# A hybrid decoder step: a projection's remainders on VectorE, its stores a block later, two rooms exchanged and one room each for two sums of weights

## The chip, the cores and the metric

The kernel runs on one core of one Trainium2 chip. A core has a matrix engine (TensorE, PE in the profile, with its weight loads as PEld), three engines for elementwise work (VectorE or DVE, ScalarE or ACT, GpSimd or POOL) and SyncE (SP), which only issues DMAs here. Each engine runs its own list of instructions in order and waits on semaphores for the others. The metric is the device time of one execution in microseconds (us). Three runs of the kernel before gave 1149.54, 1150.51 and 1150.65 us; the median is 1150.51 us.

## The reference

The reference is one step of a decoder with one layer: 1024 new tokens of a prompt behind 16 meta tokens, and 8 running sequences with 4 new tokens each, 1072 columns in all; the model width is 1024. In short:

```python
u = rmsnorm(h, g) @ w_in                  # q, k, v, gate, conv input, dt
mix = concat(window_attention(q, k, v), mamba2_ssd(conv(xbc), dt))
h = h + norm_and_gate(mix) @ w_out        # output projection
a = relu(rmsnorm(h, g2) @ w_up) ** 2      # 1024 -> 4096
h = h + a @ w_down                        # 4096 -> 1024
y = rmsnorm(h, g_final)
```

All of it is in float32, and the caches and states are outputs too.

## The kernel before, in words

Activations lie with features on the 128 partitions and tokens along the free dimension. Every float32 operand `x` of a large product is split into a rounded `hi` and a remainder `lo = x - hi`, and a product is three products on PE: `hi*hi`, `hi*lo`, `lo*hi`. So each block of weights goes through a load (SyncE), a cast to `hi` (ScalarE) and a subtraction for `lo` (VectorE or GpSimd) before PE can use it. These are `load_wout` (lines 240, 243 and 244 in it) for the output projection and `split_w` (lines 1252 and 1253) for the MLP. Tiles called `whi`, `wlo` and `w7x` are six rooms that take the split weights in turn.

The stages, by the time in the trace: input projection and attention (to about 305 us), the state-space part together with the first half of the output projection (to about 414 us), the second half of the projection, the MLP's first layer (466 to about 800 us), its second layer (to about 1134 us), and the last norm.

The output projection's columns come in three chunks (two of them 288 and 384 wide make up columns 0 to 671, the third has 384). Blocks `m` of 128 features are counted 0 to 7. In the second half, `wout_stream` runs through m and the first two chunks: `mixer_half` adds the product to `ha`, ScalarE squares it, GpSimd sums the squares in `sq`. The sum is stored to `he` in DRAM by SyncE (line 1012), and `gained` (line 970) multiplies `ha` in place by the norm's gain, which has to wait until that store has read it. `Ahead` loads two blocks of weights ahead. Then the loop `for m in range(8)` does the third chunk in the same way with VectorE for its sums and remainders, and between its blocks runs the norms of chunks 0 and 1 in steps (`norms2`, `token_norm`): sum over features on PE (`c`), the reciprocal root, a diagonal matrix `dg` on VectorE (line 1223), and its spread over partitions by PE.

The MLP's layers use a scheme with seven products instead of eight for 2 x 2 blocks (j = 1 to 7); some need sums or differences of weight blocks, made in `prep_up`: `S = a21 + a22` for j=5, `S - a11` for j=6, `a11 - a21` for j=7, `a12 - S` for j=3. The 16 output pairs p run one after the other. For the first six ("early" pairs), j=1 and j=2 are computed ahead of the rest, while the second half of the operands is still being made; their relu-squared result `b11` is stored from GpSimd's queue (line 1342), and the main steps (5, 6, 7, 4, 3) follow later. In a main step, j=6 and j=7 go on adding to the same two banks; after each, ScalarE copies the banks out (`copies`, line 1310, tiles `s2` and `s3`). The next product into a bank has to wait for that copy. VectorE adds copies and banks to the outputs `u` (line 1315). `prepare` keeps the weights of four steps ahead.

The rooms `s2` and `s3` have one buffer each and serve `b11` of the early pairs first. `S` has two buffers; `a11 - a21` is written into the place of the loaded `a21`.

A scheduler orders each engine's instructions within what the dependences allow, so the order in the trace is not the order of the code. `final_last` at the end of the program normalises the last columns and has six idle matmuls ahead of the last spread.

Of the kernel before, what the change touches and what calls it, by code (L numbers as in the profile page):

```python
# [9 lines left out]
F32 = mybir.dt.float32  # L10
# [181 lines left out]
def body(ctx: ExitStack, tc: tile.TileContext, xT, xm, win, wdt, wo, wu, wd, ck, cv, sc, st, sT, vec, consts,  # L192
# [54 lines left out]
    class Ahead:  # L247
# [9 lines left out]
        def next(self):  # L257
            while self.fns and len(self.got) <= self.n:
                self.more()
            return self.got.pop(0)  # L260
# [633 lines left out]
    kv_s.close()  # L894


    weights = Ahead([lambda m=m, half=half: load_wout(m, half) for half in range(2) for m in range(8)], 2)
    weights.more()
    hd = dram.tile([128, 8, TM], F32, name="hd")
    he = dram.tile([128, 8, TM], F32, name="he")  # L900
# [67 lines left out]
    def gained(m, out, x):  # L968

        ACT.activation(out=out, in_=x, func=AF.Copy, scale=vec[:, V_G2 + m:V_G2 + m + 1])  # L970
# [3 lines left out]
    def wout_stream():  # L974

        ws = {}
        for m, ch in [(0, 0), (0, 1), (1, 0), (1, 1), (0, 2), (1, 2)] + [(m, ch) for m in range(2, 8) for ch in range(3)]:
            c0, cw = CM[ch]
            if m not in ws:
                ws[m] = weights.next()  # L980
            hb = sp.tile([128, 384], F32, name="hb", tag="hb", bufs=3)[:, :cw]
            SP.dma_start(out=hb, in_=xm[:, 8 * c0 + m * cw:8 * c0 + (m + 1) * cw])
            ps = gps()
            gemm(ps[:, :cw], ws[m], X[ch])
            DVE.tensor_tensor(out=hb, in0=hb, in1=ps[:, :cw], op=ALU.add)
            SP.dma_start(out=hd[:, m, c0:c0 + cw], in_=hb)
            yield
        acta_s.close()
        opb = act_s.enter_context(pool("opb", side="right"))

        ha = xn["ha"] = opb.tile([128, 8, TM], F32, name="ha")
        c2 = CM[2][0]
        first = [load_kept(0, ch, sp) for ch in range(2)]
        SP.dma_start(out=ha[:, 1], in_=hd[:, 1])
        SP.dma_start(out=ha[:, 2], in_=hd[:, 2])
        SP.dma_start(out=ha[:, 0, c2:], in_=hd[:, 0, c2:])
        for m in range(3, 8):
            SP.dma_start(out=ha[:, m], in_=hd[:, m])
        sq01 = opb.tile([128, CM[2][0]], F32, name="sq01")
        sq.update({ch: sq01[:, CM[ch][0]:CM[ch + 1][0]] for ch in range(2)})  # L1000
        pieces = [(m, ch) for m in range(8) for ch in range(2)]
        for m, ch in pieces:
            c0, cw = CM[ch]
            if ch == 0:
                w = weights.next()
            hb = ha[:, m, c0:c0 + cw] if m else first[ch]
            mixer_half(m, ch, w, hb, sp, POOL)
            if m == 0:
                SP.dma_start(out=he[:, m, c0:c0 + cw], in_=hb)
                gained(m, ha[:, m, c0:c0 + cw], hb)  # L1010
            elif ch == 1:
                SP.dma_start(out=he[:, m, 0:c2], in_=ha[:, m, 0:c2])
                if m > 1:
                    gained(m - 1, ha[:, m - 1, 0:c2], ha[:, m - 1, 0:c2])
            yield
        gained(7, ha[:, 7, 0:c2], ha[:, 7, 0:c2])

    def xcols(i):
        if i == 0:
# [255 lines left out]
    def prep_up(p, j, first):  # L1275

        g = p if p < NPRE and j in (1, 2) else NPRE + p
        if first:
            load_up(g + 2)
            if g == len(groups) - 1:  # L1280
                load_first((0, 1))
        a11, a12 = raws[g, 0][:, 0:4], raws[g, 0][:, 4:8]
        if g >= NPRE:
            a21, a22 = raws[g, 1][:, 0:4], raws[g, 1][:, 4:8]
        tt = DVE.tensor_tensor
        if j == 5:
            S_[p] = pu.tile([128, 4, 128], F32, name="S", tag="S", bufs=2)
            tt(out=S_[p], in0=a21, in1=a22, op=ALU.add)
        elif j == 6:
            tt(out=S_[p], in0=S_[p], in1=a11, op=ALU.subtract)  # L1290
        elif j == 7:
            tt(out=a21, in0=a11, in1=a21, op=ALU.subtract)
        elif j == 3:
            tt(out=a12, in0=a12, in1=S_[p], op=ALU.subtract)
        src = {5: lambda: S_[p], 1: lambda: a11, 2: lambda: a12, 6: lambda: S_[p], 7: lambda: a21, 4: lambda: a22, 3: lambda: a12}[j]()
        wts[p, j] = split_w(pu, "w7x", src)

    OPN = {1: "b11", 2: "b21", 3: "b22", 4: "t4", 5: "t1", 6: "t2", 7: "t3"}
# [32 lines left out]
    def run_up(p, j):  # L1331
        pre = p < NPRE
        if pre and j == 1:
            chain[p, "a"] = [bank("b" if p % 2 else "g") for _ in range(2)]
            product(chain[p, "a"], p, 1, True)
            s_[p, 1] = copies("s1", chain[p, "a"], 2)
            POOL.dma_start(out=s1d[p], in_=s_[p, 1])
        elif pre and j == 2:
            product(chain[p, "a"], p, 2, False)
            b = pu.tile([128, 2, TQ], F32, name="b11", tag="s2" if p % 2 else "s3", bufs=1)  # L1340
            relu2_of(b, chain[p, "a"])
            POOL.dma_start(out=u7[p][:, 4], in_=b.rearrange("p c t -> p (c t)"))
        elif j == 5:
            us[p] = pu.tile([128, 4, TH], F32, name="u", tag="u", bufs=2)
            if pre:
                s_[p, 1] = pu.tile([128, 2, TQ], F32, name="s1", tag="s1", bufs=2)
                SP.dma_start(out=s_[p, 1], in_=s1d[p])
                chain[p, "a"] = [bank("g") for _ in range(2)]
                for c in range(2):
                    ACT.copy(out=chain[p, "a"][c][:, :TQ], in_=s_[p, 1][:, c])  # L1350
                SP.dma_start(out=us[p][:, 0], in_=u7[p][:, 4])
            chain[p, "b"] = [bank("b") for _ in range(2)]
            product(chain[p, "b"], p, 5, True)
        elif j == 1:
            chain[p, "a"] = [bank("g") for _ in range(2)]
            product(chain[p, "a"], p, 1, True)
            s_[p, 1] = copies("s1", chain[p, "a"], 2)
        elif j == 2:
            cc = [bank("c") for _ in range(2)]
            product(cc, p, 2, True)  # L1360
            sums(quad(p, 0), cc, s_[p, 1])
            relu2(us[p][:, 0], 0)
        elif j in (6, 7):
            product(chain[p, "a"], p, j, False)
            s_[p, j] = copies("s2" if j == 6 else "s3", chain[p, "a"])
            if j == 7:
                sums(quad(p, 2), chain[p, "b"], s_[p, 7])
                relu2(us[p][:, 2], 1)
        elif j == 4:
            product(chain[p, "a"], p, 4, False)  # L1370
            relu2_of(quad(p, 1), chain[p, "a"])
        else:
            product(chain[p, "b"], p, 3, False)
            sums(quad(p, 3), chain[p, "b"], s_[p, 6])
            relu2(us[p][:, 3], 1)
            u, t = us[p], pu.tile([128, 4, TH], F32, name="t", tag="x", bufs=2)
            tt = DVE.tensor_tensor
            tt(out=t[:, 0], in0=u[:, 3], in1=u[:, 0], op=ALU.subtract)
            tt(out=t[:, 2], in0=u[:, 2], in1=u[:, 3], op=ALU.subtract)
            tt(out=t[:, 1], in0=u[:, 2], in1=t[:, 0], op=ALU.subtract)  # L1380
            tt(out=t[:, 3], in0=u[:, 1], in1=t[:, 1], op=ALU.subtract)
            a = 1 if pre else 0
            POOL.dma_start(out=u7[p][:, 4 + a:7], in_=u[:, a:3])  # L1383
            POOL.dma_start(out=u7[p][:, 0:4], in_=t)
# [71 lines left out]
    for m in range(8):  # L1456
        w = ahead
        if m < 7:
            ahead = weights.next()
        mixer_half(m, 2, w, bs[:, m, c2:], nw, DVE)  # L1460
        POOL.dma_start(out=he[:, m, c2:], in_=bs[:, m, c2:])
        gained(m, xn["b22" if m > 3 else "b12"][:, m % 4, c2 - TH:], bs[:, m, c2:])
        if m < 6:
            next(norms2[m // 3], None)
        if m in (0, 2):
            operand(xa, "b21" if m else "b11")
            split_op("b21" if m else "b11", bs[:, 2 * m:2 * m + 4, 0:TH])
        elif m == 3:
            for n, name in enumerate(("b12", "b22")):
                ACT.copy(out=xn[name][:, :, 0:CM[2][0] - TH], in_=bs[:, 4 * n:4 * n + 4, TH:c2])  # L1470
            prepare(1)
        elif m == 4:
            DVE.tensor_tensor(out=xn["b11"], in0=xn["b12"], in1=bs[:, 0:4, 0:TH], op=ALU.subtract)
            prepare(2)
        elif m == 5:
            ACT.copy(out=xn["b21"], in_=bs[:, 4:8, 0:TH])
# [238 lines left out]
    def final_last():  # L1715
# [17 lines left out]
        pt = sum_tokens("c", q2[:, 3])  # L1733

        for _ in range(6):
            mm(idle2[:, 0:128], ones, ones, True, True)
        rs = hpool.tile([128, 3], F32, name="rs3", tag="rs3", bufs=2)
        DVE.scalar_tensor_tensor(out=rs, in0=pt[:, 0:3], scalar=1.0 / D, in1=part, op0=ALU.mult, op1=ALU.add)
        POOL.tensor_tensor(out=rs, in0=rs, in1=nhalf[:, 0:3], op=ALU.pow)
# [67 lines left out]
```

## Time and profile before

| | us |
|---|---|
| median of three runs | 1150.51 |
| the profiled execution | 1149.81 |
| its span on the engines | 1147.9 |
| PE busy | 1115.6 |
| VectorE busy | 842.9 |
| ScalarE busy | 568.7 |
| GpSimd busy | 243.9 |

The profile is of one execution. Its span is counted from the first to the last instruction; 1.9 us lie around it. The mean granted clock of PE is 0.993 of its full speed. In the timeline, a row gives start and duration in us, the engine, the line, the operation with its output and input tiles, the shape and, in brackets, how long the engine had been idle before it and what released it. A line 202 is the helper that issues every matmul, so matmuls are told apart by their tiles. A line "SPq" or "POOLq" stands for the issuing of a DMA.

### The profile page before, as it was taken

How to read it: one execution, taken by the hardware profiler on the slowest of the kernel's cores; microseconds unless marked ns; L12 is line 12 of the kernel's file. 1: busy time of each engine (PE TensorE's matmuls, PEld its weight loads, DVE VectorE, ACT ScalarE, POOL GpSimd, SP SyncE). 2: the span in 40 equal slices, each digit the busy share in tenths (PEclk: the TensorE clock that was granted, in tenths of full speed). 3: DMA queues.
4: the chain of work that ended last, by engine and by line, in shares of the span. 5: the costliest groups of instructions: out<-in, count | busy, mean ns of one | idle time of the engine just before them, and what ended most of it. 6: DMA issues, size and time to landing. Idle time of an engine off the chain costs nothing.

```text
span 1147.9 us, 21812 instructions
## 1 busy us (share of the span) xinstructions
PE 1115.6 (97%) x8405; PEld 1077.4 (94%) x8405; DVE 842.9 (73%) x1665; ACT 568.7 (50%) x1195; POOL 243.9 (21%) x307
## 2 busy tenths in 40 slices
PE   9999999999989999999999999999999999999997
PEld 8989987889878899999999999999999999999996
DVE  6646888996689966988777777766589656767583
ACT  8212556565566648854444444444434334546461
POOL 0432455654434556210000000000000000000000
PEclk9999999999999999999999999999999999999999
DMA  8131110111466576656544243433999654465273
GB/s 290 62 96 37 38 38 19 38 38 56 131 206 179 160 257 215 192 191 207 187 165 173 110 179 125 148 143 123 374 311 318 206 173 112 123 184 161 88 233 105
DMA packets 84424, 177.64 MB, mean 155 GB/s; under 512 B 10692, under 2 KB 32740, under 8 KB 82272
## 3 DMA queue, kind: packets, MB, share of 16 engines
q1 hardware_dynamic: 77392, 141.58, 39.5%
q0 software_dynamic: 6224, 33.74, 7.3%
q8 instruction: 66, 1.08, 0.4%
q10 hardware_dynamic: 704, 0.93, 0.2%
q14 instruction: 38, 0.31, 0.1%
HBM read 125.49 MB, written 50.72 MB: 154 GB/s over the span
## 4 chain that ended last, share of the span: by engine, by line
PE 72%; DVE 13%; DMA 5%; ACT 4%; issue 4%; POOL 1%; POOLq 0%; DVEq 0%; SPq 0%; ACTq 0%
PE g L202 39%; PE b L202 16%; PE c L202 9%; PE s L202 3%; DMA wdr<-in_wd 2%; PE o L202 2%; DVE bc L523 1%; DMA wraw<-in_win 1%; ACT p L675 1%; PE pt L202 1%; DVE Qs L706 1%; DVE Sd L1576 1%; DVE ts L1590 1%; DMA wraw<-in_wu 1%; PE y L202 1%
## 5 line engine op out<-in xcount | busy, mean ns | idle before, releaser
L202 PE MATMUL g<-acth,whi 128*128 128x384 f32 (+2 forms) x528 | 162.2, 332 | 0.2 <-DVE qT L453 0.2
L202 PE MATMUL g<-acth,wlo 128*128 128x384 f32 (+2 forms) x528 | 160.7, 329 | 1.2 <-ACT wlo L243 0.7
L202 PE MATMUL g<-actl,whi 128*128 128x384 f32 (+2 forms) x432 | 141.5, 327 | 0.0
L1589 ACT CAST ts<-tr 128x528 fp32r<-128x528 f32 x92 | 58.2, 632 | 115.0 <-PE b L202 96.0
L1590 DVE TENSOR_TENSOR ts<-tr,ts 128x528 fp32r<-128x528 f32 x92 | 64.8, 705 | 53.5 <-ACT ts L1589 52.4
L202 PEld LDWEIGHTS g<-acth,wlo 128*128 128x128 f32 x528 | 98.1, 190 | 3.7 <-issue 1.6
L202 PEld LDWEIGHTS g<-acth,whi 128*128 128x128 f32 x528 | 97.7, 189 | 2.8 <-issue 2.0
L202 PEld LDWEIGHTS g<-actl,whi 128*128 128x128 f32 x432 | 81.9, 190 | 0.9 <-issue 0.8
L321 POOL TENSOR_TENSOR rs<-rs,nhalf 128x3 f32<-128x3 f32 x9 | 9.8, 1094 | 337.3 <-DVE rs L320 337.3
L1310 ACT COPY s<-g 128x264 f32<-128x264 f32 x90 | 33.9, 379 | 71.5 <-PE g L202 67.8
L234 POOL TENSOR_TENSOR wlo<-wraw,whi 128x256 fp32r<-128x256 f32 x56 | 49.5, 914 | 11.2 <-ACT whi L231 11.1
L1383 POOL DMA_DIRECT2D u<-u x16 | 8.5, 532 | 177.7 <-ACT u L1326 144.1
L1315 DVE TENSOR_TENSOR u<-b,s 128x264 f32<-128x264 f32 x64 | 27.3, 430 | 24.6 <-PE b L202 14.2
L1320 ACT ACTIVATE u<-u 128x528 f32<-128x528 f32 x42 | 27.1, 646 | 28.1 <-DVE u L1319 28.1
L202 PE MATMUL b<-ts,w7y 128*128 128x264 f32 x279 | 39.3, 285 | 0.0
L732 POOL TENSOR_TENSOR p<-p,sm 128x512 f32<-128x512 f32 (+1 forms) x32 | 33.8, 1077 | 25.3 <-DVE sm L730 15.6
L202 PE MATMUL g<-ts,whi 128*128 128x264 f32 x279 | 38.9, 284 | 0.0
L202 PE MATMUL g<-ts,w7y 128*128 128x264 f32 x279 | 38.9, 283 | 0.0
L202 PE MATMUL b<-ts,whi 128*128 128x264 f32 x279 | 38.9, 284 | 0.0
L202 PE MATMUL g<-ts,wlo 128*128 128x264 f32 x270 | 38.0, 285 | 0.0
L202 PE MATMUL b<-ts,wlo 128*128 128x264 f32 x270 | 37.3, 283 | 0.0
L675 ACT ACTIVATE p<-p,nm 128x256 f32<-128x256 f32 (+1 forms) x64 | 31.3, 490 | 10.5 <-DVE nm L673 10.4
(578 smaller groups left out, 3510.5 us busy)
## 6 DMA issues: line engine op xcount, KB each, us to landing
tr<-u SPq DMA_DIRECT2D x92, 264.0 KB, 3.1
wraw<-in_wu SPq DMA_DIRECT2D x38, 512.0 KB, 4.0
wdr<-in_wd SPq DMA_DIRECT2D x68, 256.0 KB, 3.7
u<-t POOLq DMA_DIRECT2D x16, 1056.0 KB, 5.5
wraw<-in_win SPq DMA_DIRECT2D x16, 512.0 KB, 3.8
u<-u POOLq DMA_DIRECT2D x10, 792.0 KB, 3.6
wraw<-in_wo SPq DMA_DIRECT2D x24, 256.0 KB, 3.0
h<-he SPq DMA_DIRECT2D x16, 264.0 KB, 5.1
```

Of the source, the lines that this page charges most:

```text
L202: PE.matmul(out, lhsT=a, rhs=b, start=start, stop=stop, skip_group_check=on)
L234: eng.tensor_tensor(out=lo[:, n], in0=raw[:, n], in1=f(hi[:, n]), op=ALU.subtract)
L523: DVE.scalar_tensor_tensor(out=acc, in0=cb[:, j:j + CL], scalar=cw_(j), in1=acc, op0=ALU.mult, op1=ALU.add)
L675: ACT.activation(out=s_out, in_=s_out, func=AF.Exp, bias=nm, scale=-1.0, accum_out=sm)
L706: DVE.tensor_tensor(out=Q[oth, g, :, :rows], in0=src, in1=f(Q[own, g, :, :rows]), op=ALU.subtract)
L732: POOL.tensor_tensor(out=p[:rows, r:r + 2, :W], in0=p[:rows, r:r + 2, :W], in1=sm[:rows, r:r + 2].unsqueeze(2).broadcast_to([rows, 2, W]), ...
L1310: ACT.copy(out=s[:, c], in_=ps[c][:, :TQ])
L1315: DVE.tensor_tensor(out=out[:, c], in0=ps[c][:, :TQ], in1=s[:, c], op=ALU.add)
L1320: ACT.activation(out=x, in_=x, func=AF.Square)
L1576: tt(out=s, in0=s, in1=r, op=ALU.subtract)
L1589: ACT.copy(out=t[:, 0], in_=x)
L1590: DVE.tensor_tensor(out=t[:, 1], in0=x, in1=f(t[:, 0]), op=ALU.subtract)
```

## The change

There are six edits.

1. `load_wout` of the second half makes the remainders of m=3 to 7 on VectorE instead of GpSimd.
2. In `wout_stream`, the store of a block to `he` is issued after the first chunk of the next block instead of after its own second chunk, and `gained` runs two blocks behind instead of one.
3. `b11` of the odd early pairs takes room `s3`, that of the even ones `s2` (before: the other way round).
4. `S` has one buffer instead of two, and `a11 - a21` has a room of its own, `S3`, instead of the place of `a21`.
5. The third step of the norms of chunks 0 and 1 (the spread) runs one block m later.
6. The six idle matmuls at the end read the last squares `q2`, so they run behind the sum over these squares.

```diff
-    weights = Ahead([lambda m=m, half=half: load_wout(m, half) for half in range(2) for m in range(8)], 2)
+    weights = Ahead([lambda m=m, half=half: load_wout(m, half, DVE if half and m > 2 else POOL) for half in range(2) for m in range(8)], 2)
...
-            elif ch == 1:
-                SP.dma_start(out=he[:, m, 0:c2], in_=ha[:, m, 0:c2])
-                if m > 1:
-                    gained(m - 1, ha[:, m - 1, 0:c2], ha[:, m - 1, 0:c2])
+            elif ch == 0 and m > 1:
+                SP.dma_start(out=he[:, m - 1, 0:c2], in_=ha[:, m - 1, 0:c2])
+            elif ch == 1 and m > 2:
+                gained(m - 2, ha[:, m - 2, 0:c2], ha[:, m - 2, 0:c2])
             yield
-        gained(7, ha[:, 7, 0:c2], ha[:, 7, 0:c2])
+        SP.dma_start(out=he[:, 7, 0:c2], in_=ha[:, 7, 0:c2])
+        for m in (6, 7):
+            gained(m, ha[:, m, 0:c2], ha[:, m, 0:c2])
...
         if j == 5:
-            S_[p] = pu.tile([128, 4, 128], F32, name="S", tag="S", bufs=2)
+            S_[p] = pu.tile([128, 4, 128], F32, name="S", tag="S", bufs=1)
             tt(out=S_[p], in0=a21, in1=a22, op=ALU.add)
         elif j == 6:
             tt(out=S_[p], in0=S_[p], in1=a11, op=ALU.subtract)
         elif j == 7:
-            tt(out=a21, in0=a11, in1=a21, op=ALU.subtract)
+            S3 = pu.tile([128, 4, 128], F32, name="S3", tag="S3", bufs=1)
+            tt(out=S3, in0=a11, in1=a21, op=ALU.subtract)
         elif j == 3:
             tt(out=a12, in0=a12, in1=S_[p], op=ALU.subtract)
-        src = {5: lambda: S_[p], 1: lambda: a11, 2: lambda: a12, 6: lambda: S_[p], 7: lambda: a21, 4: lambda: a22, 3: lambda: a12}[j]()
+        src = {5: lambda: S_[p], 1: lambda: a11, 2: lambda: a12, 6: lambda: S_[p], 7: lambda: S3, 4: lambda: a22, 3: lambda: a12}[j]()
...
-            b = pu.tile([128, 2, TQ], F32, name="b11", tag="s2" if p % 2 else "s3", bufs=1)
+            b = pu.tile([128, 2, TQ], F32, name="b11", tag="s3" if p % 2 else "s2", bufs=1)
...
-        if m < 6:
-            next(norms2[m // 3], None)
+        for n in range(2):
+
+            if m - 3 * n in (0, 1, 3):
+                next(norms2[n], None)
...
-            mm(idle2[:, 0:128], ones, ones, True, True)
+            mm(idle2[:, 0:128], q2[:, 3, 0:128], ones, True, True)
```

The scheduler's order changes with it. In SyncE's list the rows below are the stores of `he` (line 1009 for m=0, 1012 for the others) and the loads of the projection's weights (line 240), from the first store on. Before:

```order
L1009 DMA he_3324<-hb_4756 128x288 [waits DMAHW2_49,DVE_49]
L1009 DMA he_3324<-hb_4758 128x384 [waits DMAHW3_49,DVE_49]
L1012 DMA he_3324<-ha_4755 128x672 [waits DMAHW4_49,DVE_49]
L1012 DMA he_3324<-ha_4755 128x672 [waits DMAHW5_49,DVE_49]
L240 DMA wraw_4897<-in_wo 128x512 [waits DMAHW6_49,Pool_49]
L1012 DMA he_3324<-ha_4755 128x672 [waits DMAHW7_49,DVE_49]
```

After, the same stretch of its list:

```order
L1009 DMA he_3324<-hb_4756 128x288 [waits DMAHW2_49,DVE_49]
L1009 DMA he_3324<-hb_4758 128x384 [waits DMAHW3_49,DVE_49]
L1012 DMA he_3324<-ha_4755 128x672 [waits DMAHW4_49,DVE_49]
L240 DMA wraw_4895<-in_wo 128x512 [waits DMAHW5_49,Activation_49]
L1012 DMA he_3324<-ha_4755 128x672 [waits DMAHW6_49,DVE_49]
L240 DMA wraw_4936<-in_wo 128x512 [waits DMAHW7_49,Activation_49]
```

The load of m=5 (the first of line 240 here) moves in front of the store of block 2, and the one of m=6 in front of the store of block 3.

VectorE's list at the change from one early pair to the next, where the trace of before has the row at 570.82 us. `S_6604` (before) and `S_6609` (after) belong to the same pair; line numbers after are two or three larger. Before:

```order
L1253 TENSOR_TENSOR wlo_6606<-S_6604,wlo_6606 128x512 [waits Activation_49]
L1292 TENSOR_TENSOR wraw1_6602<-wraw0_6600,wraw1_6602 128x512 [waits DMAHW4_49,DVE_49]
L1378 TENSOR_TENSOR t_6555<-u_6388 128x528 [waits DMAHW6_49,DMASW0_49,Activation_49]
L1379 TENSOR_TENSOR t_6555<-u_6388 128x528
L1380 TENSOR_TENSOR t_6555<-u_6388,t_6555 128x528 [waits DVE_49]
L1290 TENSOR_TENSOR S_6604<-S_6604,wraw0_6422 128x512
L1381 TENSOR_TENSOR t_6555<-u_6388,t_6555 128x528 [waits DVE_49]
L1294 TENSOR_TENSOR wraw0_6422<-wraw0_6422,S_6604 128x512 [waits DVE_49]
```

After, the same stretch of its list:

```order
L1255 TENSOR_TENSOR wlo_6611<-S_6609,wlo_6611 128x512 [waits Activation_49]
L1292 TENSOR_TENSOR S_6609<-S_6609,wraw0_6426 128x512 [waits DVE_49]
L1381 TENSOR_TENSOR t_6560<-u_6392 128x528 [waits DMAHW6_49,DMASW0_49,Activation_49]
L1382 TENSOR_TENSOR t_6560<-u_6392 128x528
L1383 TENSOR_TENSOR t_6560<-u_6392,t_6560 128x528 [waits DVE_49]
L1255 TENSOR_TENSOR w7x_6642<-S_6609,w7x_6642 128x512 [waits Activation_49]
L1384 TENSOR_TENSOR t_6560<-u_6392,t_6560 128x528 [waits DVE_49]
L1297 TENSOR_TENSOR wraw0_6426<-wraw0_6426,S_6609 128x512
L1290 TENSOR_TENSOR S_6788<-wraw1_6607 128x512 [waits DMAHW3_49,DVE_49]
L1255 TENSOR_TENSOR whi_6678<-S3_6676,whi_6678 128x512 [waits PE_49,Activation_49]
L1295 TENSOR_TENSOR S3_6923<-wraw0_6605,wraw1_6607 128x512 [waits DMAHW4_49,DVE_49]
L1318 TENSOR_TENSOR u_6571<-b_6579,s3_6669 128x264 [waits DMASW1_49,Activation_49]
```

The subtraction for `S` (j=6) now stands directly behind the remainder of line 1253, and the instructions that wait for the next pair's loads (`S_6788`, `S3_6923`) stand behind the sums `t` and in front of the sum `u`.

ScalarE's list at the same place: casts of weights (line 1252, after 1254) and the copies of the two banks (line 1310, after 1313). Before:

```order
L1252 CAST wlo_6606<-S_6604 128x512 [waits PE_49,Activation_49]
L1320 ACTIVATE u_6388<-u_6388 128x528 [waits DVE_49]
L1310 COPY s2_6633<-g_6569 128x264 [waits PE_49,Activation_49]
L1252 CAST w7x_6637<-S_6604 128x512 [waits DVE_49]
L1310 COPY s2_6633<-g_6570 128x264 [waits PE_49]
```

After, the same stretch of its list:

```order
L1254 CAST wlo_6611<-S_6609 128x512 [waits PE_49,Activation_49]
L1323 ACTIVATE u_6392<-u_6392 128x528 [waits DVE_49]
L1254 CAST w7x_6642<-S_6609 128x512 [waits DVE_49,PE_49,Activation_49]
L1313 COPY s2_6638<-g_6574 128x264 [waits PE_49,Activation_49]
L1313 COPY s2_6638<-g_6575 128x264 [waits PE_49]
```

The cast of `S` for j=6 moves from between the two copies to in front of both.

## Rows read from the trace of the kernel before

**Rows 1.** The page, busy time, share of the span and instructions of each engine.
```profile
PE 1115.6 (97%) x8405; PEld 1077.4 (94%) x8405; DVE 842.9 (73%) x1665; ACT 568.7 (50%) x1195; POOL 243.9 (21%) x307
```
**Rows 2.** PE's waits in 430-500, 500-580, 580-1110, 1110-1150 us: total, times, longest.
```profile
PE c L202 <- DVE dg L1223: 1.7, 2, 1.2
...
PE g L202 <- ACT s L1310: 4.1, 2, 2.2
...
PE c L202 <- DVE h L1446: 0.5, 2, 0.3
...
PE c L202 <- DVE dg L1630: 1.3, 1, 1.3
```
**Rows 3.** Timeline of PE, 434 to 465 us: start, duration, instruction, idle before.
```profile
434.59 0.41 PE L202 MATMUL g<-acth,wlo 128*128 128x288 f32 x1 [0.72 <-ACT wlo L243]
...
435.95 0.54 PE L202 MATMUL g<-acth,wlo 128*128 128x288 f32 x2 [0.48 <-POOL wlo L244]
...
464.19 0.91 PE L202 MATMUL c<-dg,ones 128*128 128x128 f32 x6 [1.15 <-DVE dg L1223]
```
**Rows 4.** Timelines of ScalarE, VectorE and GpSimd, 433 to 446 us.
```profile
433.17 0.86 ACT L970 ACTIVATE ha<-ha,vec 128x672 f32<-128x672 f32 x1 [0.21 <-DMA he<-ha]
433.93 0.60 ACT L243 CAST wlo<-wraw 128x512 fp32r<-128x512 f32 x1
...
433.90 0.55 DVE L960 TENSOR_TENSOR ha<-ha,g 128x384 f32<-128x384 f32 x1 [1.63 <-PE g L202]
...
442.59 1.10 DVE L244 TENSOR_TENSOR whi<-wraw,whi 128x512 fp32r<-128x512 f32 x1
...
444.96 0.69 DVE L244 TENSOR_TENSOR wlo<-wraw,wlo 128x512 fp32r<-128x512 f32 x1 [0.81 <-ACT wlo L243]
...
434.61 1.28 POOL L244 TENSOR_TENSOR wlo<-wraw,wlo 128x512 fp32r<-128x512 f32 x1 [0.76 <-ACT wlo L243]
```
**Rows 5.** Stretch; PE, PEld, DVE, ACT, POOL busy (count), granted clock, DMA share, GB/s.
```profile
459.70:474.00 14.30, 13.15 (x94) 12.80 (x92) 14.30 (x21) 11.76 (x22) 4.16 (x6) 1.00 0.74 225
480.00:490.00 10.00, 10.00 (x84) 9.99 (x83) 10.00 (x13) 9.76 (x15) 1.41 (x3) 1.00 0.49 165
```
**Rows 6.** The chain of waits, 500 to 516 us: start, duration, what.
```profile
507.06 5.14 DMA u<-b
```
**Rows 7.** Timelines of GpSimd, ScalarE, PE and VectorE, 500 to 516 us.
```profile
501.94 0.54 POOL L1342 DMA_DIRECT2D u<-b  x1 [3.78 <-ACT b L1326]
...
512.30 0.66 ACT L1310 COPY s<-g 128x264 f32<-128x264 f32 x2 [3.66 <-DMA u<-b]
...
512.73 0.39 PE L202 MATMUL g<-xt3h,w7x 128*128 128x264 f32 x1 [1.87 <-ACT s L1310]
...
513.85 0.69 DVE L1292 TENSOR_TENSOR wraw<-wraw,wraw 128x512 f32<-128x512 f32 x1 [2.92 <-DMA wraw<-in_wu]
```
**Rows 8.** Chain of waits (first row) and timelines of VectorE, ScalarE, PE, 563-576 us.
```profile
563.97 6.76 DMA wraw<-in_wu
...
567.03 0.68 DVE L1253 TENSOR_TENSOR wlo<-S,wlo 128x512 fp32r<-128x512 f32 x1
...
570.82 0.69 DVE L1292 TENSOR_TENSOR wraw<-wraw,wraw 128x512 f32<-128x512 f32 x1 [3.10 <-DMA wraw<-in_wu]
...
574.01 0.62 ACT L1252 CAST w7x<-S 128x512 fp32r<-128x512 f32 x1 [3.73 <-DVE S L1290]
...
574.96 0.39 PE L202 MATMUL g<-xt3h,wlo 128*128 128x264 f32 x1 [2.24 <-ACT s L1310]
```
**Rows 9.** Busy time by stretch, as in rows 5, behind the two waits.
```profile
513.00:520.00 7.00, 7.00 (x60) 7.00 (x60) 4.64 (x9) 3.83 (x9) 0.00 (x0) 1.00 0.07 10
576.40:578.00 1.60, 1.60 (x10) 1.60 (x9) 1.16 (x3) 0.90 (x2) 0.00 (x0) 0.53 0.99 399
578.00:580.00 2.00, 2.00 (x12) 2.00 (x11) 0.94 (x3) 0.80 (x2) 0.00 (x0) 0.52 0.75 317
```
**Rows 10.** Timeline of PE at the end.
```profile
1136.42 1.28 PE L202 MATMUL g<-ones 128*128 128x128 f32 x10
```

## The prediction, made before the change was run

> **What bounds the kernel now.** I read the busy time by engine first: TensorE (PE) works for 1115.6 us of a span of 1147.9 us [rows 1], so nothing but its 32 us of gaps, and stretches at a lower clock, can be won. Then I read PE's waits by stretch. The change has a hand only behind 420 us, and there the waits named are few, about 9 us of the 32: before 500 us 1.7 us for `dg` and 1.2 us for the projection's weights [rows 2, 3], 4.1 us in two waits between 500 and 580 us, both for the copies `s` of line 1310, 0.5 us from 580 to 1110 us, and 1.3 us at the end [rows 2]. Third I read PE's timeline around each of them, fourth what stood ahead of the late instruction on its own engine (the timelines of ScalarE, VectorE and GpSimd, and the chain of waits), and last the granted clock behind each wait. Since PE waits only 0.5 us between 580 and 1110 us, a microsecond saved ahead of that comes out at the end.
>
> **The projection (edits on the weights, the stores and the norm).** Block m=5 of the second half makes PE wait twice: 0.72 us for the rounded weights and 0.48 us for their remainder [rows 3]. On ScalarE the cast stood behind `gained` (line 970), which had waited for a store of `he` to land; it ran at 433.93 and took 0.60 us. GpSimd then took 1.28 us for the remainder [rows 4]. After the change the stores are issued a block later and `gained` two blocks later; the load of m=5 passes one store in SyncE's queue, and its cast passes `gained` on ScalarE (both in the order). ScalarE was free 0.21 us before `gained` started at 433.17 [rows 4], so the cast can run from 432.96 to 433.56 us, and the first of the two waits goes. VectorE makes the same remainder in 0.69 us, behind its add that runs at 433.90 for 0.55 us [rows 4]: 434.45 + 0.6 to 0.7 = 435.1 us, against the 435.95 us at which PE goes on now [rows 3]. Gain 0.85 us of the 1.20 us; the bounds are 0 and 1.2 us.
>
> Five remainders come to VectorE, 5 x 0.69 = 3.4 us, in a stretch where it still has pauses (it waited 1.63 us before the add [rows 4]). Beside a GpSimd instruction the same operation took 1.10 us [rows 4]; that price would make it 435.5 us and the gain 0.4 us. The Trainium skill ("SBUF — State Buffer", section "Who interferes with whom") says that a VectorE instruction with two inputs in SBUF and a GpSimd instruction that reads SBUF exclude each other for a whole instruction. Each remainder and each of GpSimd's remaining sums (line 966) are such a pair. The row of 1.10 us agrees in direction; by that rule a collision would cost up to a whole GpSimd sum, and the gain at m=5 would be about nothing.
>
> What is won there must still get past the wait of 1.15 us at 464.19 us for `dg` [rows 3]. It belongs to VectorE, which is busy for 14.30 of 14.30 us from 459.7 us on [rows 5]. Moving the norm's step one block later puts three 384-column matmuls, 0.5 us, ahead of the waiting one, which turns 0.5 us of that wait into work done earlier, but not into a later start of VectorE. So what passes on is what VectorE's own chain gains, 0.5 to 0.75 us from fewer and earlier steps. I take 0.7 us for the three edits together, bounds 0 (the loads decide everything; a weight load of the next stage now stands in front of one of the projection's) and 1.6 us.
>
> **The exchanged rooms.** The first copy `s2` of main pair 0 could not start before the store of pair 5's `b11` had read that room: the store was issued at 507.06 us and took 5.14 us, ScalarE waited 3.66 us for that store and PE 1.87 us for the copy [rows 6, 7]. With the rooms exchanged `s2` shares with pair 4, whose store was issued at 501.94 us [rows 7]; with the same 5.14 us it has landed by 507.1, over 2 us before it is wanted. The copy `s3` now waits for pair 5's store, to 512.2 us, and PE wants it one step later: a step is 24 matmuls, 60 of which go in 7.00 us [rows 9], so 2.8 us. Without the wait the product that needs `s3` out of its bank would start at 512.73 - 1.87 + 2.8 = 513.7 us; the store's 512.2 and a copy of about 0.4 us (two in 0.66 [rows 7]) make 512.6 us. The margin is 1.1 us, and I take the whole gain of 1.87 us (bounds 0 and 1.87).
>
> **One room each for S and S3.** The wait of 2.24 us at 574.96 us [rows 8] is a chain through two queues. VectorE had the subtraction for the next pair's seventh product (line 1292, in place) early in its order; it stood 3.10 us for a load issued at 563.97 us that took 6.76 us [rows 8]. Behind it came three sums `t` and then `S` (line 1290) of the pair before, which needed no new load. ScalarE had the cast of that `S` between the two copies `s`: it waited 3.73 us, to 574.01 [rows 8], and the second copy, for which PE waited, ran after it. In the new order VectorE makes `S` directly behind the remainder of line 1253, before the sums and before any instruction that waits for a load, which ran at 567.03 and took 0.68 us [rows 8]: at 567.7 to 568.4 us; the cast on ScalarE comes before both copies. PE then gets the copy when its bank is done. Gain 2.24 us (bounds 0 and 2.24). What is late next is the new `S3`: the sums of the layer's outputs are queued behind it on VectorE, and PE's fifth product of a pair waits for those. In pair 0 the in-place version stood until 513.85 [rows 7]; plus 0.69 us, a remainder of 0.6 and a sum of 0.4 us is about 515.5 us, and PE, two products of 2.8 us behind 510.86 us, asks at 516.5 us. The margin is 1.0 us. From pair 6 on, `S` for the next pair is made later than now, but still several products ahead.
>
> **The clock.** After this second wait PE ran at a granted clock of 0.53 and 0.52 for 3.60 us, that is at 1.2 GHz instead of 2.4 [rows 9]. At full clock the same work is 1.60 x 0.53 + 2.00 x 0.52 = 1.89 us. So 1.71 us more hang on the wait. After the first one, of 1.87 us, the clock stayed at 1.00 [rows 9]. If the second wait goes, I take the whole 1.7 us (bounds 0, if the fall comes from elsewhere, and 1.7).
>
> **The end.** The six idle matmuls now run behind the sum of squares instead of in front of it. Ten small matmuls took 1.28 us [rows 10], so six take 0.8 us, inside the 1.3 us that PE waits there for `dg` [rows 2]. Nothing, from -0.1 to +0.2 us.
>
> **The sum.** 0.7 + 1.87 + 2.24 + 1.7 = 6.5 us. The profiled execution took 1149.81 us (span 1147.9 and 1.9 around it), so it would take 1143.3; it lies 0.7 us under the median of 1150.51, and from the median I get 1144.0 us.
>
> **Rivals.**
> 1. *Only the room and the projection pay* (0.13). The second wait comes back in another form: the cast waits for its room, or `S` again comes too late, and the clock falls with it. For it: ScalarE's queue has casts and copies in one order, and any late cast there stops a copy. Against it: the new order has `S` free of loads. 1150.5 - 0.7 - 1.87 = 1147.9 us.
> 2. *The loads only change the instruction that they stop* (0.14). The loads of the up-projection's weights and the stores share the transfer engines, and if every product starts earlier while the loads land when they do now, PE meets them a step later; or the edits do not do what they say, because the store of pair 5 lands over 1.1 us later. For it: loads of 5 to 7 us as in [rows 8]; against it: PE waits for none of them from 580 us on [rows 2]. The gain left is 0 to 2 us: 1149.5 us.
> 3. *Slower: `S3` before the sums* (0.08). One room for `S` and for `S3` puts the subtraction that waits for a load ahead of the output sums in every early pair. The longest stand of VectorE for such a load is 3.10 us [rows 8]; were the loads later by that everywhere, 3.1 - 1.0 = 2.1 us would reach PE in each of five pairs: 10.5 us, and 1144.0 + 10.5 = 1154.5 us. It decides once the loads land more than 1.0 us later than in pair 0 now; slower than today it is from 2.3 us on. VectorE has no slack to make up for it in the stage before (busy 10.00 of 10.00 us from 480 us [rows 5]). Against it: today's waits for loads on VectorE reached PE once in six pairs [rows 2], and the loads are not issued later than now.
>
> **How the numbers follow.** The forecast has 0.65; its own range, with the clock's and the projection's bounds, is 1142.6 to 1146.5 us. Rival 1 ends at 1147.9. The low end cannot pass 1150.5 - (1.6 + 1.87 + 2.24 + 1.7) = 1143.1 us by more than the spread of the runs, so the range is 1142.6 to 1148.6 us; above it lie rival 3 and most of rival 2. A change of 0.2%, 2.3 us, is about what a measurement of this kernel can tell from none. Faster by more: the forecast and rival 1, a part of rival 2, 0.80. Within it: 0.12. Slower: rival 3, 0.08.
>
> **What would show it.** Right: PE's waits for `s` of line 1310 gone between 500 and 580 us, the granted clock 1.00 throughout 570 to 582 us, `S` on VectorE made before the sums `t`, the cast of m=5 not behind `gained`, PE's wait there under 0.5 us. Wrong: a wait of over 1 us for a sum `u` or `b` at the fifth product of an early pair (rival 3), a cast named as what PE or a copy waits for (rival 1), or a wait for `s3` of pair 0. If the wait goes and the clock falls all the same, the time is 1145.7 us.

## The result, and the profile after

The changed kernel took 1141.62 us (median of four runs, 1140.08 to 1144.12), the kernel before beside it 1150.03 us; the ratio is 0.9929, with an interval of 0.9906 to 0.9951. The forecast was 1144.0 us with a range of 1142.6 to 1148.6 us: the direction is right, the gain between these medians is 8.4 us instead of 6.5, and the measured median lies 1.0 us below the range. The profiled execution took 1142.43 us, 7.4 us less than the one before, with a span of 1140.4 us, 7.5 us less.

The page of the kernel after, busy time by engine, answers to [rows 1]:

```profile
PE 1113.5 (98%) x8405; PEld 1075.9 (94%) x8405; DVE 849.5 (74%) x1670; ACT 568.7 (50%) x1195; POOL 237.2 (21%) x302
```

TensorE has the same 8405 matmuls and is busy for 2.1 us less; 1.7 us of that is the price of the stretch at the low clock behind the second wait, which is gone. VectorE has five instructions more and GpSimd five fewer. PE's waits after, in 430-500, 580-1110 and 1110-1150 us; from 500 to 580 us there is none ([rows 2] had 4.1 us there):

```profile
PE c L202 <- DVE dg L1225: 1.5, 2, 1.0
PE g L202 <- DVE wlo L244: 0.6, 1, 0.6
...
PE c L202 <- DVE h L1449: 0.3, 1, 0.3
...
PE c L202 <- ACT q L1737: 1.0, 1, 1.0
PE c L202 <- DVE dg L1635: 0.2, 1, 0.2
```

VectorE and ScalarE after, at the change from pair 4 to pair 5 (timelines), answer to [rows 8]:

```profile
564.25 0.69 DVE L1255 TENSOR_TENSOR wlo<-S,wlo 128x512 fp32r<-128x512 f32 x1
564.97 0.69 DVE L1292 TENSOR_TENSOR S<-S,wraw 128x512 f32<-128x512 f32 x1
...
570.70 0.69 DVE L1295 TENSOR_TENSOR S<-wraw,wraw 128x512 f32<-128x512 f32 x1
571.31 0.43 DVE L1318 TENSOR_TENSOR u<-b,s 128x264 f32<-128x264 f32 x1
...
566.12 0.62 ACT L1254 CAST w7x<-S 128x512 fp32r<-128x512 f32 x1 [1.11 <-PE b L202]
567.59 0.38 ACT L1313 COPY s<-g 128x264 f32<-128x264 f32 x1 [0.84 <-PE g L202]
568.99 0.38 ACT L1313 COPY s<-g 128x264 f32<-128x264 f32 x1 [1.01 <-PE g L202]
```

`S` for j=6 is made right behind the remainder, its cast runs 1.5 us ahead of the first copy, and both copies wait for nothing but their bank. `S3` (570.70) has its load when its turn comes and goes straight on into the sum `u`. The stretches after, PE's busy time and the granted clock as in [rows 9]:

```profile
568.00:572.00 4.00, 4.00 (x35) 4.00 (x35) 3.67 (x7) 1.39 (x4) 0.53 (x1) 1.00 0.53 144
572.00:576.00 4.00, 4.00 (x35) 4.00 (x35) 3.00 (x6) 2.85 (x6) 0.00 (x0) 1.00 0.54 207
576.00:580.00 4.00, 4.00 (x35) 4.00 (x35) 2.85 (x6) 1.30 (x3) 0.53 (x1) 1.00 0.79 181
```

The simplest measure of this part of the program is the time from the first matmul of one pair's fifth product (`b<-xt1h`) to that of the next pair, read off PE's timeline. An early pair that waits for nothing takes 14.55 to 14.58 us.

| profile of | pair 0 | pairs 1 to 3 | pair 4 | pair 5 |
|---|---|---|---|---|
| before | 16.69 | 14.56-14.57 | 18.61 | 14.75 |
| after | 14.56 | 14.55-14.58 | 14.57 | 14.58 |

So in these two profiles 6.3 us of the 7.5 us of span come from pairs 0, 4 and 5; the forecast's terms for them were 1.87 + 2.24 + 1.7 = 5.8 us.

### The profile page after: what moved, and what is told of

Same layout as the page of the kernel before. It is cut to its first block, busy times and chain, and to the rows that moved or that the text cites. A ratio compares the mean times of both kernels' runs of the same rounds, so it can differ in the third digit from the quotient of the medians.

```text
span 1140.4 us, 21840 instructions
## 1 busy us (share of the span) xinstructions
PE 1113.5 (98%) x8405; PEld 1075.9 (94%) x8405; DVE 849.5 (74%) x1670; ACT 568.7 (50%) x1195; POOL 237.2 (21%) x302
## 4 chain that ended last, share of the span: by engine, by line
PE 76%; DVE 12%; ACT 4%; DMA 4%; issue 3%; POOL 1%; POOLq 0%; SPq 0%; DVEq 0%; ACTq 0%
PE g L202 40%; PE b L202 19%; PE c L202 9%; PE s L202 3%; PE o L202 2%; DMA wdr<-in_wd 1%; DVE bc L523 1%; DMA wraw<-in_win 1%; ACT p L675 1%; PE pt L202 1%; DVE Qs L706 1%; DMA hd<-hb 1%; PE y L202 1%; PE pt L742 1%; DVE p L673 1%
```

## Experiments

Times are medians. A ratio is to runs of the kernel before, taken beside it on the same chip, with its 95% interval; gains in us are worked out from the ratio.

**The changed kernel again.** No edit.

> The changed kernel once more, against the kernel before. Theory (the terms 0.7 + 1.87 + 2.24 + 1.7 = 6.5 us are the change, and what was measured beyond them is the granted clock at places that the change does not touch, which differs from run to run): 6 to 7.5 us faster, times of single runs from 1140 to 1144 us that go down as the run's mean clock goes up, and a spread in the kernel before of the same kind. Rival (the change gains about 2 us more than its terms somewhere): 8 us or more again, at any clock.

1141.77 us (6 runs, 1139.89 to 1144.29) against 1148.69 us (29 runs, 1145.37 to 1152.87): 0.9946, 0.9926 to 0.9966, or 6.2 us (3.9 to 8.5).

> The changed kernel a third time, beside the kernel with one more remainder on VectorE. Theory: 5.5 to 7 us faster than before, with single runs from 1140 to 1144 us; no wait of PE between 500 and 580 us, and every early pair of the first layer in 14.55 to 14.58 us. Rival (the 8.4 us of the first comparison are the change): 8 us or more.

1141.21 us (6 runs, 1138.98 to 1143.65) against 1148.45 us (17 runs): 0.9934, 0.9919 to 0.9949, or 7.6 us (5.9 to 9.3). That is above the 5.5 to 7 us expected and below the rival's 8 us, and the interval reaches into both. All early pairs took 14.55 to 14.58 us in both profiles. The kernel after repeats; it was the kernel before that came out lower: 75 runs of it, on three chips, lie between 1145.12 and 1154.66 us with a mean of 1148.73, where the three runs that the forecast started from gave 1149.54 to 1150.65. The 16 runs of the changed kernel have a mean of 1141.70. The difference of the means is 7.0 us, with an interval of about 0.9 us to either side by the spread of these runs.

Single runs differ by several microseconds, and the difference goes with the mean granted clock of each. In 58 of those runs of the kernel before, the 11 at 0.996 took 1146.1 us on average, the 23 at 0.993 took 1149.5 and the 3 at 0.990 took 1152.0: about 1.1 us for each 0.001. Profiles show low stretches at 100 to 108 us in 7 of 14 executions (in one more at 21 to 25 us), and between 308 and 332 us in all, outside the change's reach.

**One room each for S and S3, alone.**

```diff
-            S_[p] = pu.tile([128, 4, 128], F32, name="S", tag="S", bufs=2)
+            S_[p] = pu.tile([128, 4, 128], F32, name="S", tag="S", bufs=1)
...
-            tt(out=a21, in0=a11, in1=a21, op=ALU.subtract)
+            S3 = pu.tile([128, 4, 128], F32, name="S3", tag="S3", bufs=1)
+            tt(out=S3, in0=a11, in1=a21, op=ALU.subtract)
```

> The kernel before with one room each for S and S3 and nothing else. Theory: the wait of 2.24 us at 575 us and the low clock behind it go, 3.9 us faster (3.5 to 4.3); the wait of 1.87 us at 512.7 us stays. Rival (the clock falls for reasons of its own): the wait goes, a stretch at about 0.5 stays between 570 and 582 us, 2.2 us faster. Second rival (S3 ahead of the sums costs): PE waits for a sum u or a bank b in an early pair.

0.9967 (0.9952 to 0.9982), 3.8 us (2.1 to 5.5). Pair 4 takes 14.57 us, the clock stays at 1.00 there, and nothing waits for a sum `u`. The wait of pair 0 stays, at 1.1 us in this profile.

**Half of that: S in one buffer, a21 still overwritten.**

```diff
-            S_[p] = pu.tile([128, 4, 128], F32, name="S", tag="S", bufs=2)
+            S_[p] = pu.tile([128, 4, 128], F32, name="S", tag="S", bufs=1)
```

> The kernel before with S in one buffer, and a11 - a21 still in the place of a21: half of the edit on the sums of weights. VectorE's order comes out as in the changed kernel (S directly behind the remainder of line 1253). Theory (what ends the wait at 575 us is S before the instructions that wait for loads, not the room S3): 3.9 us faster, like both halves together. Rival (S3's own room is needed): the wait stays or comes back elsewhere between 500 and 600 us.

0.9970 (0.9957 to 0.9984), 3.4 us, and pair 4 again in 14.57 us. VectorE's timeline in this kernel:

```profile
568.72 0.69 DVE L1290 TENSOR_TENSOR S<-S,wraw 128x512 f32<-128x512 f32 x1
...
574.34 0.69 DVE L1292 TENSOR_TENSOR wraw<-wraw,wraw 128x512 f32<-128x512 f32 x1
```

A single number, fewer buffers, does it: the subtraction of line 1292, which stood for a load in front of `S` ([rows 8]), now comes 5.6 us behind it and waits for nothing. With one buffer the next pair's `S` cannot be made before this pair's has been used. The subtraction overwrites `a21`, which that next `S` reads, so it has to stay behind too. The room `S3` adds nothing that these runs can tell.

**The rooms of b11 exchanged, alone.**

```diff
-            b = pu.tile([128, 2, TQ], F32, name="b11", tag="s2" if p % 2 else "s3", bufs=1)
+            b = pu.tile([128, 2, TQ], F32, name="b11", tag="s3" if p % 2 else "s2", bufs=1)
```

> The kernel before with the rooms of b11 exchanged and nothing else. Theory: the wait at 512.7 us goes, 1.9 us faster; the wait of 2.2 us behind it and the low clock there stay, 1.9 us earlier. Rival (the wait moves to s3): PE waits about 1 us for s3 at 514 us and the gain is under 1 us. If the clock falls because of both waits together, it stays at 1.00 here and the gain is 3.6 us.

0.9976 (0.9961 to 0.9990), 2.8 us (1.1 to 4.5). Pair 0 takes 14.56 us, and no wait for `s3` comes in its place. PE's timeline and the stretches around the other wait in this kernel:

```profile
570.02 0.39 PE L202 MATMUL g<-xt3h,wlo 128*128 128x264 f32 x1 [1.84 <-ACT s L1310]
...
570.00:576.00 6.00, 5.98 (x49) 5.99 (x50) 4.92 (x10) 3.76 (x8) 0.48 (x1) 1.00 0.74 244
```

Here the wait is there and the clock does not fall: pair 4 takes 16.72 us, not 18.61. That is what was expected for the case that the fall needs both waits; one profile, and a gain that fits 1.9 us as well as 3.6, do not decide it.

**Both of them, without the projection and the end.** The edits of the two single kernels above.

> The kernel before with the rooms of b11 exchanged and one room each for S and S3, without the edits on the projection and on the end. Theory: the terms add up, 1.87 + 2.24 + 1.7 = 5.8 us faster, PE has no wait between 500 and 580 us. Rival (each part alone leaves something to the other): more or less than the sum by over 0.7 us.

0.9950 (0.9933 to 0.9967), 5.7 us (3.8 to 7.7): the sum that was expected, and no wait between 500 and 580 us.

**The idle time of pair 4 filled.** In the kernel before, ahead of the matmul that waits:

```diff
         for c in range(2):
+            if (p, j, c) == (4, 7, 1):
+                fill = bank("c")
+                for _ in range(16):
+                    mm(fill[:, 0:128], s_[p, 6][:, 0, 0:128], ones, True, True)
             for k in range(4):
```

> The kernel before with 16 matmuls of 128 columns, whose result nobody reads, in front of the matmul that waits at 575 us: PE waits for the same copy but is busy meanwhile (16 x 0.13 = 2.1 of 2.24 us). Theory (the low clock comes from PE's idle time): the granted clock stays at 1.00 from 570 to 582 us, the next product starts when it does now, and the kernel is 1.7 us faster without any wait removed. Rival (the clock falls for another reason): stretch at about 0.5 stays, same time within 0.3 us.

0.9998 (0.9984 to 1.0011): no change, and not the 1.7 us of the theory. The 16 matmuls took 3.5 us instead of 2.1, because the 0.13 us was the time of one record, and each of these float32 matmuls stands as two records in the profile (32 for the 16). They held up the product for 1.4 us after the copy was there (pair 4: 18.15 us), but the clock stayed at 1.00. With `range(9)` in place of `range(16)`:

> The kernel before with 9 instead of 16 unread matmuls in front of the one that waits at 575 us. The 16 took 3.5 us, 0.22 each, over 1 us more than the wait; 9 take 2.0 us and end before the copy is there. Theory (idle time takes the clock down, and it does so there in some of the runs): granted clock 1.00 from 570 to 582 us, pair 4 of the first layer takes 14.56 + 2.2 = 16.8 us, on average 0.5 to 1.7 us faster than before. Rival: a stretch at about 0.5 stays, pair 4 takes over 18 us.

0.9982 (0.9967 to 0.9998), 2.1 us. PE's timeline, and two stretches, in this kernel:

```profile
572.67 2.17 PE L202 MATMUL c<-ones,s 128*128 128x128 f32 x18
575.29 0.39 PE L202 MATMUL g<-xt3h,wlo 128*128 128x264 f32 x1 [0.45 <-ACT s L1314]
...
570.00:576.00 6.00, 5.55 (x47) 5.36 (x46) 4.84 (x8) 2.04 (x5) 0.53 (x1) 1.00 0.05 13
576.00:582.00 6.00, 6.00 (x52) 6.00 (x51) 4.71 (x10) 3.02 (x7) 0.51 (x1) 1.00 0.82 274
```

The product starts when the copy is there, as before, with 2.2 us of useless work in a wait of 2.6 us, and the clock stays up: pair 4 takes 17.31 us. The interval of 0.2 to 3.8 us fits the expected 0.5 to 1.7. This speaks for PE's idle time as the cause of the fall; two profiles without a fall, beside three falls in five where the wait was not filled, do not show it.

**The three edits on the projection, alone** (remainders, stores and gains, norm step, as in the change).

> The kernel before with the remainders on VectorE, the stores and the gains a block later and the norm's step a block later (three edits). Theory: 0.7 us faster at the first product behind the projection (bounds 0 and 1.6), and the waits at 512.7 and 575 us stay. Rival (these edits carry what was measured beyond the forecast): 2 us faster or more.

0.9993 (0.9979 to 1.0008): 0.8 us (0.9 slower to 2.4 faster), not told from none. In its profile the wait of pair 0 is 2.69 us, and this time the clock falls behind it (and not behind the one of pair 4, 2.0 us). Two stretches:

```profile
512.00:514.00 2.00, 1.98 (x12) 1.98 (x13) 1.01 (x2) 0.77 (x2) 0.00 (x0) 0.71 0.00 0
514.00:516.00 2.00, 2.00 (x11) 2.00 (x11) 0.43 (x1) 0.38 (x1) 0.00 (x0) 0.50 0.00 0
```

**Only the remainders on VectorE** (first line of the change's diff).

> The kernel before with the remainders of m=3 to 7 on VectorE, and the stores, gains and norm steps as before. Question: which edit moves the two waits at m=5, of 0.4 to 0.7 us for the cast and 0.5 us for the remainder. Theory: the first wait stays (the cast still stands behind the gain, which waits for a store), the second shrinks from 0.5 us to under 0.2 us, since VectorE needs 0.7 instead of 1.3 us. Rival (VectorE's own queue makes the remainder as late): the second wait stays at about 0.5 us or above, and the remainder on VectorE is worth nothing without the later stores.

A single run of 1152.03 us, beside one of 1144.83 us of the kernel before. The two say nothing on 0.5 us, since in that execution the clock fell behind both waits. At m=5, PE's timeline:

```profile
434.61 0.40 PE L202 MATMUL g<-acth,wlo 128*128 128x288 f32 x1 [0.40 <-ACT wlo L243]
...
435.46 0.54 PE L202 MATMUL g<-acth,wlo 128*128 128x288 f32 x2
```

The first wait stays, and the second is gone, as expected. In the kernels that have the stores moved as well it is the other way round: no first wait and 0.64 to 0.65 us in the second ([rows 3] had 0.72 and 0.48). PE gets to the remainder sooner and waits there instead, for the remainder is ready 1.2 us after the start of VectorE's add either way. From PE's last matmul in front of these waits to its going on it is 1.6 us in this profile and in the one after. So at m=5 the remainder on VectorE is what counts, and the later stores add nothing there. Alone it did not carry through, though: in this one profile PE waits another 0.66 us for the sum of squares on GpSimd (line 966) at 448.9 us, and the stage is no shorter than without the edits.

**The idle matmuls at the end, alone.**

```diff
-            mm(idle2[:, 0:128], ones, ones, True, True)
+            mm(idle2[:, 0:128], q2[:, 3, 0:128], ones, True, True)
```

> The kernel before with the six idle matmuls at the end behind the last sum of squares. Theory: no change, within 0.3 us; PE's wait for dg shrinks from 1.3 to 0.3 us, and a wait for the squares takes its place. Rival (the end is 0.4 us shorter for it): 0.4 us faster, with the spread or what follows it earlier against the last product.

1.0006 (0.9992 to 1.0020): no change. PE's waits at the end are those of the changed kernel:

```profile
PE c L202 <- ACT q L1732: 1.0, 1, 1.0
PE c L202 <- DVE dg L1630: 0.2, 1, 0.2
```

Together they are about what the 1.3 us were.

**One more remainder on VectorE.** In the changed kernel, as the traces of all kernels show VectorE's `R` (line 935) late and the clock low behind it:

```diff
-    load_wout(m, half, DVE if half and m > 2 else POOL)
+    load_wout(m, half, DVE if (half, m) == (0, 4) or half and m > 2 else POOL)
```

> The changed kernel with one more remainder on VectorE: that of block m=4 of the first half, which GpSimd made at 321.9 us for 1.25 us while VectorE's second product R (line 935) took up to 2.75 us against 1.1 in the median. Theory (the two exclude each other, R waits for GpSimd's remainder): R ends about 1.2 us earlier, PE's two waits for R shrink from 3.0 to about 1.8 us, 1.2 us faster than the changed kernel, and where the clock then stays up another 1 to 1.7. Rival (R waits for the other GpSimd instructions of that stretch, or something else is late for the product): PE's wait there stays within 0.3 us and the time is that of the changed kernel.

1139.50 us (5 runs, 1138.21 to 1142.10), ratio to before 0.9921 (0.9906 to 0.9937). Beside it the changed kernel took 1141.21 us at 0.9934 (0.9919 to 0.9949); it is the fastest kernel here, but the intervals of the two overlap. VectorE and GpSimd in the third run of the changed kernel, then in this one (timelines):

```profile
319.25 4.44 DVE L935 TENSOR_TENSOR R<-tm,cs 128x512 fp32r<-128x512 f32 x2
...
318.57 1.90 POOL L1122 TENSOR_TENSOR Bm<-BS,cs 96x1024 fp32r<-96x1024 f32 x1 [1.96 <-DVE BS L1107]
320.43 1.49 POOL L1082 TENSOR_TENSOR hn<-hn,ex 128x512 f32<-128x512 f32 x1
321.88 1.25 POOL L244 TENSOR_TENSOR whi<-wraw,whi 128x512 fp32r<-128x512 f32 x1
```

```profile
317.75 3.09 DVE L935 TENSOR_TENSOR R<-tm,cs 128x512 fp32r<-128x512 f32 x2
...
316.79 1.90 POOL L1122 TENSOR_TENSOR Bm<-BS,cs 96x1024 fp32r<-96x1024 f32 x1 [1.96 <-DMA hd<-hb]
318.65 1.04 POOL L1082 TENSOR_TENSOR hn<-hn,ex 128x512 f32<-128x512 f32 x1
```

Without GpSimd's third instruction the two `R` take 1.35 us less; PE's wait for them goes from 3.0 to 1.9 us, as expected. The clock still falls behind the wait that is left. The `R` one by one, the second of the changed kernel and then both of this one:

```profile
320.94 2.75 DVE L935 TENSOR_TENSOR R<-tm,cs 128x512 fp32r<-128x512 f32 x1
```

```profile
317.75 2.49 DVE L935 TENSOR_TENSOR R<-tm,cs 128x512 fp32r<-128x512 f32 x1
...
320.16 0.68 DVE L935 TENSOR_TENSOR R<-tm,cs 128x512 fp32r<-128x512 f32 x1
```

The `R` with nothing from GpSimd beside it takes 0.68 us. The ones of 2.75 and 2.49 us end about 0.55 us after GpSimd's last instruction in both kernels (at 323.69 us behind 321.88 + 1.25 = 323.13, and at 320.24 behind 318.65 + 1.04 = 319.69). The Trainium skill ("SBUF — State Buffer", section "Who interferes with whom") states that a VectorE instruction with two inputs in SBUF contends with a GpSimd instruction that reads SBUF; these rows agree.

## Why the prediction was right, and where it was wrong

**The exchanged rooms: right.** 1.87 us were forecast. In the eight profiles that still have that wait it is 1.07 to 2.70 us, 1.74 on average. Pair 0 takes 1.4 to 4.5 us more than 14.57 us there, 2.4 on average, with a low clock behind the wait in two of them; in all profiles with the exchange it takes 14.56 or 14.57, and `s3` is never waited for.

**S and S3: right in the mechanism, and half of the edit is idle.** 2.24 us without the clock. The chain of load, sums `t`, `S`, cast and copy is gone as described; rival 1 (another late cast) and rival 3 (`S3` ahead of the sums) do not appear in any profile. Nor does rival 2 (another instruction stopped by the loads): PE has no wait between 500 and 580 us with both edits, and 0.3 us at most from 580 to 1110 us. The step named S and S3 together; S alone does it.

**The clock: right in size on average, wrong as a fixed price.** The forecast took 1.7 us for the low clock behind the second wait and nothing for the first. PE's waits, read off its timelines, and whether the granted clock fell right behind them:

| profile of | wait of pair 0, us | clock | wait of pair 4, us | clock |
|---|---|---|---|---|
| before | 1.87 | 1.00 | 2.24 | falls |
| idle_only | 1.47 | 1.00 | 2.03 | falls |
| proj_only | 2.70 | falls | 1.99 | 1.00 |
| rem_only | 1.76 | falls | 2.34 | falls |
| rooms_only | none | 1.00 | 1.84 | 1.00 |
| sums_only | 1.10 | 1.00 | none | 1.00 |
| s_one | 1.07 | 1.00 | none | 1.00 |
| filler | 2.31 | 1.00 | filled | 1.00 |
| filler9 | 1.65 | 1.00 | filled | 1.00 |

The clock fell behind the wait of pair 0 in 2 of 8 profiles, behind the one of pair 4 in 3 of 5. Where the wait was filled it fell in neither of two, and where there was none (the places marked so, and the three profiles of the changed kernel, `both` and `m4_rem`) it never fell. With (2/8 + 3/5) of such a fall at about 1.7 us each, it is 1.4 us on average: nearly the same sum, spread over two places, and different from run to run. That the sum fits is in part luck. What decides on a fall is not shown. All five falls are in profiles with both waits; a fall behind pair 0 cannot hang on a wait that comes 60 us later, but for the one behind pair 4 only `rooms_only` speaks on it.

**The projection: the mechanism holds at m=5, the size was too large.** 0.7 us were forecast. From the last matmul of the state-space part at 418 us to the first of pair 0, eight profiles without the three edits take 85.3 to 86.2 us, mean 85.9; five with them 85.2 to 86.3, mean 85.6: 0.3 us, less than the profiles of either kind differ among themselves. At m=5 the forecast of 0.85 us is what the profiles before and after show. VectorE and PE after:

```profile
434.34 0.55 DVE L960 TENSOR_TENSOR ha<-ha,g 128x384 f32<-128x384 f32 x1 [1.63 <-PE g L202]
434.81 0.69 DVE L244 TENSOR_TENSOR wlo<-wraw,wlo 128x512 fp32r<-128x512 f32 x1
...
435.56 0.54 PE L202 MATMUL g<-acth,wlo 128*128 128x288 f32 x2 [0.65 <-DVE wlo L244]
```

From the start of VectorE's add to PE's going on it is 1.22 us, against 2.05 before ([rows 3, 4]): 0.83 us less. But the two waits of 1.20 us together in the profile before were the largest of their kind; they are 0.9 us in six of the eight profiles without the edits. From PE's last matmul in front of them to its going on it is 2.4 us in the profile before, 2.1 to 2.3 in the other seven, and 1.6 in all five with the edits: 0.6 us less on average. From there to pair 0 it is 69.2 us on average with the edits and 69.0 without, but 68.4 to 70.0 in single profiles, so a loss of 0.2 us behind it is not told from none. At `dg`, where the forecast's lower bound had it, none shows: the first of these waits is 0.7 to 1.8 us in the profiles with the edits and 0.5 to 1.7 in those without, 1.1 and 1.2 us on average.

**The end: right in the result, wrong in the working.** There is no change. But [rows 10] were read as ten matmuls, where each of the six idle ones stands as two records. They take 1.58 us, not 0.8, which is more than the 1.3 us they were to fit into:

```profile
1131.20 1.58 PE L202 MATMUL g<-ones,q 128*128 128x128 f32 x12
```

It cost nothing: from the end of the last product to the spread it is 3.5 us before, after and in `idle_only`. PE now waits 1.0 us for the squares in front of the six, and 0.2 us for `dg` behind them.

**The step that failed is the base, in "How the numbers follow".** The terms were taken off the median of three runs, 1150.51 us. The low end was set with the sentence that the time cannot pass 1143.1 us "by more than the spread of the runs", and 0.5 us was allowed for that, where the three runs differ by 1.1 us. Over 75 runs the kernel before has a mean of 1148.73 us and a spread of 9.5 us: the base was 1.8 us too high, and the spread far too small. The sum of 6.5 us lies within the 7.0 us, give or take 0.9, between the means; 1148.7 - 6.5 = 1142.2 us would have been the forecast, and a range moved by as much would have held the result. The first comparison's 8.4 us between medians is the same change seen from a base 1.3 us above that mean. Three runs out of these 75 can well come out so high, as 29 of them are at 1149.54 us or above; that it was no more than that draw is not shown.

That the sum fits is in part luck, too, for its terms are off to either side. Against 14.57 us, pair 0 takes 2.4 us more on average, pair 4 3.3 us where its wait is not filled, and pair 5 0.1 us, clock included; with 0.3 us for the projection that is 6.1 us. Another 0.3 us stand at the end and were not forecast: from the start of the last spread by PE to the end of the span it is 7.4 us in the five profiles with all three of the projection's edits and 7.9 us in seven of the other nine (7.7 us in `rem_only`; 8.6 in `s_one`, where the clock is low by then), while 0.2 us more lie outside the span (2.0 against 1.8 us). Why is open. The rest is less than the runs can tell.

## What to carry to other kernels

When an engine's list of work is made by a scheduler, one more buffer can be a loss: it lets an instruction that waits for a transfer go in front of one that doesn't. Look for a wait behind which an engine does work that was ready all along, and take away the buffer that allowed the order. And before a forecast of half a per cent, look at the granted clock of each run: three runs that agree do not give the spread of a kernel whose clock falls in some executions only.

## What was not expected of the hardware

- Whether the clock falls behind a wait of about 2 us differs from run to run, and the length alone does not decide it: it fell after waits of 1.8, 2.0, 2.2, 2.3 and 2.7 us, and stayed up after others of 1.1 to 2.3 us.
- With nine matmuls of 128 columns in float32, 0.24 us each, in a wait of 2.6 us the clock stayed at 1.00; they stand as 18 in the profile. A count or a mean of such records is not one of matmuls.
- A wait for the same transfer, in the same order of work, took PE between 1.1 and 2.7 us from one profile to another (pair 0).
